# A one-core hybrid attention layer: turning the meta columns behind their step's keys, a mask operand in the first scans, and the last plain gate tiles' weights ahead of the seven-product stage

## The chip, the cores and the metric

The kernel runs on one NeuronCore of a Trainium2 chip. The metric is the device time of one execution in microseconds. The engines that matter are TensorE (PE, and PEld for its weight loads), VectorE (DVE), ScalarE (ACT), GpSimd (POOL) and SyncE (SP), which issues all the DMAs.

## The reference

One decoder layer over 2048 tokens of 1024 features, with 16 learned meta tokens ahead of them. A combined projection gives the queries, keys and values of two attention branches and four sets of gate columns. The first branch is stick-breaking attention with 8 heads: the weight of a key is its sigmoid times the running product of (1 - sigmoid) over all keys between it and the query. The second is sliding-window attention. The branches are gated, projected, merged, and projected out.

```python
xn = rms_norm(h, norm_gain[l])
proj = xn @ w_in[l]
sb_q, sb_k, sb_v, sw_q, sw_k, sw_v, sb_z, sw_z, g_sb, g_sw = jnp.split(proj, offsets, axis=-1)
...
z = jnp.einsum('bqhd,bkhd->bhqk', q[:, q0:end], k[:, :end]) * scale
mask = (s[None, :] < t[:, None]) & valid[None, :end]
log_beta = jax.nn.log_sigmoid(z)
log_1m = jnp.where(mask, log_beta - z, 0.0)
rev = lax.cumsum(log_1m, axis=3, reverse=True)
suffix = jnp.concatenate([rev[..., 1:], jnp.zeros_like(rev[..., :1])], axis=-1)
w = jnp.where(mask, jnp.exp(log_beta + suffix), 0.0)
...
y_sb = (o_sb * jax.nn.silu(sb_z)) @ w_branch_sb[l]
y_sw = (o_sw * jax.nn.silu(sw_z)) @ w_branch_swa[l]
merged = jax.nn.sigmoid(g_sb) * y_sb + jax.nn.sigmoid(g_sw) * y_sw
h = h + merged @ w_out[l]
```

## The kernel before

**Numbers.** Every float32 matrix product is three products of rounded parts: each operand is split into a high part and a low part, and the matmuls are high x high, high x low and low x high. `split` (L105) makes the parts of a weight tile: ScalarE copies the high part (L108) while `hsplit` is set, and VectorE or, while `vsplit` is off, GpSimd subtracts the low part (L111). `evac_split` (L113) does the same with a PSUM bank, ScalarE first (L114), VectorE behind it (L115).

**Order.** The tokens stand in reversed order, so that the running product over the keys is a scan from left to right. They are four groups of 512, worked on in two halves. TensorE's order is the order of the program text. A scheduler orders VectorE, ScalarE, GpSimd and SyncE, except in a few blocks where ScalarE's order is that of the text too; the plain tiles named below are such a block. `weave` mixes two streams on TensorE: projection tiles as the main one, attention steps as the side one.

**Stages of the profiled execution.** To 86 us the start; to 395 us projections and the window attention of the first half; 395 to 640 us the stick-breaking attention of the first half, woven with gate tiles; 640 to 692 us three *plain* gate tiles (`PLAIN`); 692 to 806 us twelve gate tiles (`FAST`) as six pairs by a scheme of seven products; then to 1200 us the window attention and to about 1700 us the stick-breaking attention of the second half, and the final projections.

**A stick step.** `stick` goes through steps of 512 keys by 128 queries (`steps`: head, group, key block n, query tile j). The step s runs `row` for step s, which has two key matmuls (L839) into a bank "z", ScalarE's sigmoid (L843), in the diagonal block (n = 0) a select on GpSimd that sets the masked keys to 1 (L848), and VectorE's scan (L850), the running product. At the last keys of the sequence the 16 meta columns don't fit the bank of 512, so a second pair of matmuls (L841) puts them into the bank "zm", and a second sigmoid (L845) reads that. Five steps (`LT`) later `turn` transposes the rows on TensorE (L861, bank "t", two buffers) and splits them, and `turn_meta` transposes the meta columns of a group's four rows (L872) into the same one bank "zm" and splits that into `wm`. Two steps behind, `values` takes the entries of `av_todo` in order and multiplies by the values (L887, bank "o"); the entry marked `last` ends the sum, which ScalarE and GpSimd read out (L892 to L895). In the step in which a group's last transpose is due, `turn_meta` runs first, then `row`, then `turn`.

**Gate tiles.** A gate tile is 24 matmuls for each group of 512 tokens (`gemm`, L403 to L405) into a bank "g" (two buffers), then ScalarE's sigmoid (L558), for some tiles a product on VectorE (L560), and an output DMA. `lagged` puts the sigmoid of a tile behind the first matmuls of the next.

**Seven products.** `combined` (L925) makes sums of the tokens' parts: its `steps` make t2, t4 (L943 to L952) and t3 (L956), each through `put` (L922 ScalarE, L923 VectorE), a bit of it ahead of each plain tile's group; its `last` puts t1 in place (L963). `pair_weights` (L968) loads and splits the weights of two gate tiles and makes their sums s1 to s4 (L974 to L982). `gate_pairs` (L988) runs, for each pair, seven products of 12 matmuls each (L1000 to L1002) in the order a11·b11, s2·t2, a12·b21, s4·b22, s1·t1, s3·t3, a22·t4, through the banks g, z and t in turn, and adds them up (L1006, the sigmoid is L1009). The weights of the next pair are made at the start of a pair.

Of the kernel before, what the change touches and what calls it, by code (L numbers as in the profile page):

```python
# [7 lines left out]
F32 = mybir.dt.float32  # L8
# [3 lines left out]
ALU = mybir.AluOpType  # L12
# [4 lines left out]
P = 128  # L17
# [5 lines left out]
RW = GT + NM  # L23
NB = SEQ // P
EPS = 1e-6
LT = 5
# [21 lines left out]
def tile_kernel(ctx, tc, x, xt, meta, metat, gain, w_in, w_sb, w_sw, w_out, sinks, fgain,  # L48
# [103 lines left out]
    def drain(*gens):  # L152
        for _ in chain(*gens):
            pass
# [623 lines left out]
    def stick(groups, bp, sums_of={}):  # L778
        kt, vc = {}, {}
        rows_of = {}  # L780
        for g in groups:
# [2 lines left out]
            G.affine_select(out=w, in_=f32(w), pattern=[[-1, 4], [0, P]], compare_op=ALU.is_equal, fill=0.0,  # L784
                            base=-64 - 4 * g, channel_multiplier=1)
        av_todo = []

        def load_kv(h, g):

# [26 lines left out]
        def row(h, g, n, j):  # L816

            if n == j == 0:
                load_kv(h, g)
                state[h, g] = {"q": load_q(h, g), "last": {}}  # L820
                n1 = len(state) - 1
                for g1, ssq in list(sums_of.items())[n1 // 8:n1 // 8 + 1]:
                    i, f = divmod(n1 % 8, 2)
                    t = bp.tile([P, GT], F32, tag="q2", name="xq", bufs=2)
                    DMA(t, x[g1 * GT + i * P:g1 * GT + (i + 1) * P, f * GT:(f + 1) * GT])
                    A.activation(t, t, AF.Square, accum_out=ssq[:, f, i:i + 1])
            st = state[h, g]
            last = st["last"]
            b0 = 4 * (g + n) + j
            nb = min(4, NB - b0)  # L830
            end = b0 + nb == NB
            w = nb * P + (NM if end and nb < 4 else 0)
            k0 = (b0 - 4 * groups[0]) * P
            own = end and nb == 4
            z = ps("z")
            zm = ps("zm") if own else None
            for t, qt in enumerate(st["q"]):
                lq = qt[:, j * P:(j + 1) * P]
                T.matmul(z[:, :w], lhsT=lq, rhs=kt[h][:, k0:k0 + w], start=t == 0, stop=t == 1)  # L839
                if own:  # L840
                    T.matmul(zm[:, :NM], lhsT=lq, rhs=kt[h][:, k0 + w:k0 + w + NM], start=t == 0, stop=t == 1)  # L841
            r = bp.tile([P, RW], F32, tag="row", name="row", bufs=12)
            A.activation(r[:, :w], z[:, :w], AF.Sigmoid, scale=-1.0)  # L843
            if own:
                A.activation(r[:, w:w + NM], zm[:, :NM], AF.Sigmoid, scale=-1.0)  # L845
                w += NM
            if n == 0:
                G.affine_select(out=r[:, :P], in_=r[:, :P], pattern=[[1, P]], compare_op=ALU.is_ge,  # L848
                                fill=1.0, base=-1, channel_multiplier=-1)
            V.tensor_tensor_scan(r[:, :w], r[:, :w], r[:, :w], last[j] if n else 1.0, op0=ALU.mult, op1=ALU.min)  # L850
            last[j] = r[:, w - 1:w]
            rows_of[h, g, n, j] = r

        def turn(h, g, n, i):

            i = 3 - i if n == 0 else i
            nr = i + 1 if n == 0 else 4
            tr = ps("t")
            for j in range(nr):
                k0 = (i - j) % 4 * P  # L860
                T.transpose(tr[:, j * P:(j + 1) * P], rows_of[h, g, n - (j > i), j][:, k0:k0 + P], ident)  # L861
            m = nr * P
            wh = bp.tile([P, GT], F32R, tag="wh", name="wth", bufs=3)
            wl = bp.tile([P, GT], F32R, tag="wl", name="wtl", bufs=3)
            evac_split(wh[:, :m], wl[:, :m], tr[:, :m])
            av_todo.append((h, g, vc[h, g + n][:, i, :], wh[:, :m], wl[:, :m], n == 0 and i == 3, i == (0 if g == 3 else 3) and g + n == 3))

        def turn_meta(h, g):
            p, a = divmod(h, 2)
            tr = ps("zm")  # L870
            for j in range(4):
                T.transpose(tr[:NM, j * P:(j + 1) * P], rows_of[h, g, 3 - g, j][:, GT - P * j:GT - P * j + NM], ident)  # L872
            w = wm[g % 2]
            evac_split(w[0:NM], w[32:32 + NM], tr[:NM])
            av_todo.append((h, g, vm[:, p, a, :], w, None, False, False))

        def values():

            h, g, v, wh, wl, first, last = av_todo.pop(0)
            st = state[h, g]  # L880
            if first:
                st["o"] = ps("o")
            o = st["o"]
            n = wh.shape[1]
            for r in (wh, wl):
                if r is not None:
                    T.matmul(o[:, :n], lhsT=v, rhs=r, start=first and r is wh, stop=last and r is wl)  # L887
            if last:
                p, a = divmod(h, 2)
                t = tmp(rows=64)  # L890
                u = tmp(rows=64)
                A.copy(u, o[0:64])  # L892
                A.copy(t, o[64:128])  # L893
# [5 lines left out]
        n = len(steps)  # L899
        turned = []  # L900
        for s in range(n + LT + 3):
            t = s - LT
            if 0 <= t < n and sum(steps[t][1:3]) == steps[t][3] == 3:
                turn_meta(*steps[t][:2])
                turned.append(s)
                yield 0.43
            if s < n:
                row(*steps[s])
                yield 0.45
            if 0 <= t < n:  # L910
                turn(*steps[t])
                turned.append(s)
                yield 0.43
            while av_todo and turned[0] < s - 1:
                del turned[0]
                yield values()
# [71 lines left out]
    def gate_pairs(ga, gb, pairs, pool, sums_x, between):  # L988
# [7 lines left out]
        def product(a, b):  # L996
            acc = ps("gzt"[next(banks) % 3])
            (wh, wl), (h, l) = a, b
            for k in range(HK):
                T.matmul(acc, lhsT=wh[:, k, :], rhs=h[:, k, :], start=k == 0, stop=False)  # L1000
                T.matmul(acc, lhsT=wh[:, k, :], rhs=l[:, k, :], start=False, stop=False)
                T.matmul(acc, lhsT=wl[:, k, :], rhs=h[:, k, :], start=False, stop=k == HK - 1)  # L1002
            return acc

        def add(t, acc, u):
            V.tensor_tensor(t, acc, u, op=ALU.add)  # L1006
# [2 lines left out]
            A.activation(t, t, AF.Sigmoid)  # L1009
            DMA(dst, t)  # L1010

        nxt = pair_weights(pairs[0][0], pairs[0][2], pool)
        for n, (c, cdst, d, ddst) in enumerate(pairs):
            a11, a12, a22, s1, s2, s3, s4 = nxt
            end = n + 1 == len(pairs)
            if not end:
                nxt = pair_weights(pairs[n + 1][0], pairs[n + 1][2], pool)
            p, u, v, w = (tmp() for _ in range(4))
            A.copy(p, product(a11, b11))
            add(u, product(s2, t2), p)  # L1020
            add(p, product(a12, b21), p)
            gate_out(cdst[ga], p)
            if end:
                between()
            p3 = product(s4, b22)
            p5 = product(s1, t1)
            add(v, p5, u)
            add(v, p3, v)
            gate_out(cdst[gb], v)
            add(u, product(s3, t3), u)  # L1030
            add(w, p5, u)
            gate_out(ddst[gb], w)
            add(u, product(a22, t4), u)
            gate_out(ddst[ga], u)


# [168 lines left out]
    for half, groups in enumerate(halves):  # L1205
# [45 lines left out]
        with tc.tile_pool(name=f"sb{half}", bufs=1, side="left") as bp:  # L1251
# [5 lines left out]
            cost_sb = 8 * sum(4 * (4 - g) for g in groups) * 1.31 + 16 * 0.75  # L1257
            ratio = cost_sb / ((rest - 4) * 10.4)
            weave(tiles_by_tile(gts[4:rest], groups), side, ratio)
            drain(side)  # L1260
            if half == 0:
                t, u = (bp.tile([P, GT], F32, tag="wh", name="sum", bufs=3)[:, :8] for _ in range(2))
# [4 lines left out]
                rs0, rs1 = rs[:, :4], rs[:, 4:]  # L1267
        if half == 0:
            with tc.tile_pool(name="fast", bufs=1, side="left") as bp:
                hsplit[0] = vsplit[0] = True  # L1270
                sums_x = combined(*groups, bp)
                with tc.manual_schedule(engines={mybir.EngineType.Activation}):
                    for mk in gts[rest:-FAST]:
                        w, use, _ = mk()
                        for g in groups:
                            next(sums_x[4], None)
                            drain(lagged(col_tile(w, g, use)))
                    drain(sums_x[4])
                    sums_x[5]()
                places = [(C_GSB + i * P, gs[i]) for i in range(8)] + [(C_GSW + i * P, gw[i]) for i in range(8)]  # L1280
                places = places[-FAST:]
                gate_pairs(*groups, [a + b for a, b in zip(places[::2], places[1::2])], bp, sums_x,
                           lambda: prep(halves[1][0], rs0))
                hsplit[0] = False
        else:
            ringl = rings()
# [65 lines left out]
```

## Time and profile before

| what | value |
| --- | --- |
| median of 3 runs | 2199.65 us (2198.61 to 2199.89) |
| profiled execution | 2202.32 us |
| its span, first to last instruction | 2200.3 us |
| TensorE's mean granted clock in it | 0.994 |
| TensorE busy | 2143.6 us |
| VectorE busy | 1438.8 us |
| ScalarE busy | 1083.8 us |
| GpSimd busy | 340.3 us |

The times of single instructions, waits and stages come from the one profiled execution. A row of the trace's timeline gives the start in microseconds from the start of the span, the duration, engine, line and operation, the tile written and the tiles read, and in brackets the engine's idle time before it with what ended that. A granted clock of 1 is TensorE's full speed.

### The profile page before, as it was taken

The page shows a single profiled execution, that of the slowest core. Times are in us where ns is not written, and L with a number is a line of the kernel's source. Part 1 is how long each engine was busy: PE and PEld are TensorE (multiplying, and loading weights), DVE is VectorE, ACT ScalarE, POOL GpSimd, SP SyncE. Part 2 cuts the span into 40 slices and gives each one's busy share as a digit, 9 for nine tenths or more (in the row PEclk, how much of TensorE's full clock was granted, in tenths as well). Part 3 has the DMA queues.
Part 4 walks back from the last instruction along what each step waited for, and adds up shares of the span by engine and source line. Part 5 has one row for each costly group of instructions (what it writes and reads, how often), then busy time and mean ns, then how long its engine had stood idle before and what let it go on. Part 6 is the DMA issues. An engine that isn't in the chain of part 4 may idle for free.

```text
span 2200.3 us, 30420 instructions
## 1 busy us (share of the span) xinstructions
PE 2143.6 (97%) x10542; PEld 1755.8 (80%) x10542; DVE 1438.8 (65%) x2262; ACT 1083.8 (49%) x2463; POOL 340.3 (15%) x462
## 2 busy tenths in 40 slices
PE   8999999999898999999999999999999999999998
PEld 6788888777676887888887888888888888787886
DVE  7687885567678553677664888887774436454453
ACT  6677774555554333677763555555554312221121
POOL 2233342222210000133220000000000121000000
PEclk9999999999999999999999999999999999999999
DMA  9745546654516665443436333333322985468422
GB/s 333 281 167 192 186 151 214 227 171 153 166 49 232 222 231 193 153 154 135 163 125 192 113 120 120 105 111 115 118 87 91 352 304 182 165 222 286 153 97 86
DMA packets 162617, 380.41 MB, mean 173 GB/s; under 512 B 23168, under 2 KB 24960, under 8 KB 162464
## 3 DMA queue, kind: packets, MB, share of 16 engines
q1 hardware_dynamic: 162464, 378.48, 50.0%
q8 instruction: 83, 1.36, 0.3%
q14 instruction: 70, 0.57, 0.1%
HBM read 237.35 MB, written 140.98 MB: 172 GB/s over the span
## 4 chain that ended last, share of the span: by engine, by line
PE 56%; issue 1%; ACT 1%; DVE 1%; DMA 0%; POOL 0%; SPq 0%; POOLq 0%; ACTq 0%; DVEq 0%
PE ps_g L403 6%; PE ps_g L404 6%; PE ps_g L405 6%; PE ps_o L887 5%; PE ps_z L839 4%; PE ps_t L861 4%; PE ps_g L226 1%; PE ps_g L227 1%; PE ps_z L226 1%; PE ps_z L227 1%; PE ps_z L225 1%; PE ps_g L225 1%; PE ps_o L742 1%; PE ps_z L696 1%; PE ps_t L226 1%
## 5 line engine op out<-in xcount | busy, mean ns | idle before, releaser
L403 PE MATMUL ps_g<-xh,wh 128*128 128x512 f32 x1352 | 556.5, 412 | 17.5 <-ACT wh L108 9.0
L405 PE MATMUL ps_g<-xh,wl 128*128 128x512 f32 x1352 | 533.3, 394 | 0.6 <-DVE wl L111 0.5
L404 PE MATMUL ps_g<-xl,wh 128*128 128x512 f32 x1352 | 532.9, 394 | 0.9 <-DVE xl L379 0.9
L850 DVE TENSOR_TENSOR_SCAN row<-row 128x512 f32<-128x512 f32 (+2 forms) x320 | 370.0, 1159 | 127.1 <-POOL row L848 60.1
L403 PEld LDWEIGHTS ps_g<-xh,wh 128*128 128x128 f32 x1352 | 256.5, 190 | 60.3 <-ACT wh L108 9.8
L405 PEld LDWEIGHTS ps_g<-xh,wl 128*128 128x128 f32 x1352 | 255.2, 189 | 58.8 <-DVE wl L111 1.7
L404 PEld LDWEIGHTS ps_g<-xl,wh 128*128 128x128 f32 x1352 | 256.5, 190 | 42.9 <-DVE xl L379 1.9
L843 ACT ACTIVATE row<-ps_z 128x512 f32<-128x512 f32 (+1 forms) x320 | 171.6, 537 | 193.1 <-PE ps_z L839 151.3
L115 DVE SCALAR_TENSOR_TENSOR wtl<-ps_t,wth 128x512 fp32r<-128x512 f32 (+1 forms) x320 | 188.4, 590 | 28.8 <-ACT wth L114 28.2
L114 ACT ACTIVATE wth<-ps_t 128x512 fp32r<-128x512 f32 (+1 forms) x320 | 170.3, 532 | 63.0 <-PE ps_t L861 62.3
L839 PE MATMUL ps_z<-kt,q 128*128 128x512 f32 (+3 forms) x640 | 188.7, 374 | 0.6 <-ACT row L843 0.6
L861 PE MATMUL ps_t<-ident,row 128*128 128x128 f32 x1088 | 173.5, 274 | 5.4 <-DVE wtl L115 3.1
L861 PEld LDWEIGHTS ps_t<-ident,row 128*128 128x128 f32 x1088 | 135.2, 140 | 42.0 <-DVE wtl L115 6.2
L839 PEld LDWEIGHTS ps_z<-kt,q 128*128 128x128 f32 x640 | 116.8, 189 | 23.3 <-ACT row L843 1.3
L887 PE MATMUL ps_o<-wth,vc 128*128 128x512 f32 (+1 forms) x320 | 130.6, 408 | 1.2 <-ACT tmp L893 0.9
L704 ACT ACTIVATE sc<-sc,nm 128x129 f32<-128x129 f32 x256 | 100.0, 393 | 38.0 <-DVE nm L702 37.4
L887 PE MATMUL ps_o<-wtl,vc 128*128 128x512 f32 (+1 forms) x320 | 117.4, 367 | 0.0
L848 POOL TENSOR_SCALAR_AFFINE_SELECT row<-row 128x128 f32<-128x128 f32 x128 | 44.4, 349 | 411.2 <-ACT row L843 368.3
L111 POOL TENSOR_TENSOR wl<-raw,wh 128x1024 fp32r<-128x1024 f32 (+1 forms) x28 | 60.5, 2160 | 193.2 <-ACT wh L108 176.4
L558 ACT ACTIVATE tmp<-ps_g 128x512 f32<-128x512 f32 x88 | 52.5, 597 | 75.9 <-PE ps_g L405 74.3
L108 ACT CAST wh<-raw 128x1024 fp32r<-128x1024 f32 (+1 forms) x43 | 41.6, 968 | 93.4 <-PE ps_g L226 29.9
L894 POOL TENSOR_TENSOR tmp<-tmp 64x512 f32<-64x512 f32 x32 | 42.8, 1339 | 231.3 <-ACT tmp L893 164.7
(430 smaller groups left out, 3941.6 us busy)
## 6 DMA issues: line engine op xcount, KB each, us to landing
wh<-h_in_w_in SPq DMA_DIRECT2D x66, 512.0 KB, 3.5
wl<-l_in_w_in SPq DMA_DIRECT2D x66, 512.0 KB, 4.7
raw<-in_w_in SPq DMA_DIRECT2D x50, 512.0 KB, 4.9
h_in_w_in<-wh SPq DMA_DIRECT2D x50, 512.0 KB, 2.8
l_in_w_in<-wl SPq DMA_DIRECT2D x50, 512.0 KB, 4.5
q<-qd SPq DMA_DIRECT2D x128, 128.0 KB, 3.1
vc<-vd SPq DMA_DIRECT2D x48, 256.0 KB, 3.6
kd<-tmp SPq DMA_DIRECT2D x32, 256.0 KB, 4.9
```

The source lines that it names most:

```text
L114: A.activation(h, acc, AF.Copy, scale=scale)
L115: V.scalar_tensor_tensor(l, acc, scale, f32(h), op0=ALU.mult, op1=ALU.subtract)
L226: T.matmul(acc, lhsT=wh[:, k, :], rhs=l, start=False, stop=False)
L403: T.matmul(acc, lhsT=wh[:, k, :], rhs=xh[g][:, k, :], start=k == 0, stop=False)
L404: T.matmul(acc, lhsT=wh[:, k, :], rhs=xl[g][:, k, :], start=False, stop=False)
L405: T.matmul(acc, lhsT=wl[:, k, :], rhs=xh[g][:, k, :], start=False, stop=k == KT - 1)
L704: A.activation(sc[:, hh, :], sc[:, hh, :], AF.Exp, bias=nm[:, hh:hh + 1], accum_out=den[:, hh:hh + 1])
L839: T.matmul(z[:, :w], lhsT=lq, rhs=kt[h][:, k0:k0 + w], start=t == 0, stop=t == 1)
L843: A.activation(r[:, :w], z[:, :w], AF.Sigmoid, scale=-1.0)
L850: V.tensor_tensor_scan(r[:, :w], r[:, :w], r[:, :w], last[j] if n else 1.0, op0=ALU.mult, op1=ALU.min)
L861: T.transpose(tr[:, j * P:(j + 1) * P], rows_of[h, g, n - (j > i), j][:, k0:k0 + P], ident)
L887: T.matmul(o[:, :n], lhsT=v, rhs=r, start=first and r is wh, stop=last and r is wl)
```

## The change

The change has four parts.

1. In a stick step, `turn_meta` runs behind `row` and `turn` instead of ahead of them. Its entry in `av_todo` therefore comes after that of `turn`, and it is now the one marked `last`, which ends the sum.
2. In the first half, a tile `mask` of 128 by 528 is made once: ones for the masked keys, which are those of the first 128 columns up to and with the diagonal, and zeros elsewhere. The scan of a diagonal block takes it as its second operand with a maximum, so that masked keys become 1 in the scan itself. GpSimd's select on each of these rows goes away. The second half keeps the select.
3. The weights of the first two plain tiles are loaded and split before the stick steps left over are drained, with ScalarE and VectorE doing the split, and those of the third behind the first tile. The first `pair_weights` call stands behind the third plain tile's first group instead of at the start of `gate_pairs`.
4. In `gate_pairs`, the product a22·t4 is computed ahead of s1·t1, while its sum is still added last.

```diff
+        mask = None
+        if groups[0]:
+            mask = bp.tile([P, RW], F32, name="mask")
+            V.memset(mask[:, P:], 0.0)
+            V.memset(mask[:, :P], 1.0)
+            G.affine_select(out=mask[:, :P], in_=mask[:, :P], pattern=[[-1, P]], compare_op=ALU.is_ge, fill=0.0,
+                            base=0, channel_multiplier=1)
...
-            if n == 0:
+            if n == 0 and mask is None:
                 G.affine_select(out=r[:, :P], in_=r[:, :P], pattern=[[1, P]], compare_op=ALU.is_ge,
                                 fill=1.0, base=-1, channel_multiplier=-1)
-            V.tensor_tensor_scan(r[:, :w], r[:, :w], r[:, :w], last[j] if n else 1.0, op0=ALU.mult, op1=ALU.min)
+            if n == 0 and mask is not None:
+                V.tensor_tensor_scan(r[:, :w], r[:, :w], mask[:, :w], 1.0, op0=ALU.mult, op1=ALU.max)
+            else:
+                V.tensor_tensor_scan(r[:, :w], r[:, :w], r[:, :w], last[j] if n else 1.0, op0=ALU.mult, op1=ALU.min)
...
-            av_todo.append((h, g, vc[h, g + n][:, i, :], wh[:, :m], wl[:, :m], n == 0 and i == 3, i == (0 if g == 3 else 3) and g + n == 3))
+            av_todo.append((h, g, vc[h, g + n][:, i, :], wh[:, :m], wl[:, :m], n == 0 and i == 3, False))
...
-            av_todo.append((h, g, vm[:, p, a, :], w, None, False, False))
+            av_todo.append((h, g, vm[:, p, a, :], w, None, False, True))
...
-                    T.matmul(o[:, :n], lhsT=v, rhs=r, start=first and r is wh, stop=last and r is wl)
+                    T.matmul(o[:, :n], lhsT=v, rhs=r, start=first and r is wh, stop=last)
...
         for s in range(n + LT + 3):
-            t = s - LT
-            if 0 <= t < n and sum(steps[t][1:3]) == steps[t][3] == 3:
-                turn_meta(*steps[t][:2])
-                turned.append(s)
-                yield 0.43
             if s < n:
                 row(*steps[s])
                 yield 0.45
+            t = s - LT
             if 0 <= t < n:
                 turn(*steps[t])
                 turned.append(s)
                 yield 0.43
+                if sum(steps[t][1:3]) == steps[t][3] == 3:
+                    turn_meta(*steps[t][:2])
+                    turned.append(s)
+                    yield 0.43
...
-        nxt = pair_weights(pairs[0][0], pairs[0][2], pool)
         for n, (c, cdst, d, ddst) in enumerate(pairs):
...
             p3 = product(s4, b22)
+            p4 = product(a22, t4)
             p5 = product(s1, t1)
...
-            add(u, product(a22, t4), u)
+            add(u, p4, u)
...
             weave(tiles_by_tile(gts[4:rest], groups), side, ratio)
+            if half == 0:
+                hsplit[0] = vsplit[0] = True
+                plain = [mk() for mk in gts[rest:rest + 2]]
             drain(side)
...
-                hsplit[0] = vsplit[0] = True
                 sums_x = combined(*groups, bp)
                 with tc.manual_schedule(engines={mybir.EngineType.Activation}):
-                    for mk in gts[rest:-FAST]:
-                        w, use, _ = mk()
+                    for n in range(PLAIN):
+                        w, use, _ = plain[n]
                         for g in groups:
-                            next(sums_x[4], None)
+                            if n + 1 < PLAIN:
+                                next(sums_x[4])
                             drain(lagged(col_tile(w, g, use)))
+                            if n + 1 == PLAIN and g == groups[0]:
+                                nxt = pair_weights(pairs[0][0], pairs[0][2], bp)
+                        if n + 2 < PLAIN:
+                            plain.append(gts[rest + n + 2]())
                     drain(sums_x[4])
                     sums_x[5]()
```

More of the change, by code (lines that the diff above doesn't have):

```diff
@@ L986, in pair_weights, with gate_pairs @@
                 s1, s2, s3, s4)
-    def gate_pairs(ga, gb, pairs, pool, sums_x, between):
+    def gate_pairs(ga, gb, pairs, pool, sums_x, nxt, between):
         t1, t2, t3, t4 = sums_x[:4]
```

8 lines of the change are left out of this document (4 added, 4 removed).

## The prediction

> **What bounds the kernel now.** I read the page's busy time first, then a table of stretches, then what TensorE waited for in the stretches where it is not full.
>
> ```profile
> span 2200.3 us, 30420 instructions
> ...
> PE 2143.6 (97%) x10542; PEld 1755.8 (80%) x10542; DVE 1438.8 (65%) x2262; ACT 1083.8 (49%) x2463; POOL 340.3 (15%) x462
> ```
>
> ```profile
> 395.00:640.00 245.00, 224.53 (x1197) 182.62 (x1195) 166.89 (x222) 137.06 (x306) 62.70 (x88) 0.98 0.48 158
> 640.00:692.00 52.00, 42.43 (x180) 33.48 (x180) 40.69 (x64) 21.66 (x33) 2.96 (x3) 0.90 0.35 123
> 692.00:806.00 114.00, 112.52 (x487) 90.69 (x486) 72.78 (x107) 46.33 (x71) 0.00 (x0) 1.00 0.65 232
> 1200.00:1700.00 500.00, 500.00 (x2690) 415.52 (x2689) 389.88 (x464) 274.67 (x533) 38.20 (x76) 1.00 0.34 107
> ```
>
> The second fence is the table of stretches: length, busy time of PE, PEld, DVE, ACT and POOL, granted clock, DMA share, GB/s. TensorE is the bound, 2143.6 of 2200.3 us. Only its holes can be won, 56.7 us, and what it loses at a lowered clock. 20.5 us of hole lie in the first half's stick stretch (395 to 640), 9.6 in the plain tiles (640 to 692), 1.5 in the seven-product stage, none in the second half's stick stretch (1200 to 1700). The change touches just these places. TensorE's waits from 395 to 646 (us in total, times, longest):
>
> ```profile
> PE ps_zm L841 <- DVE wm L115: 14.9, 8, 3.5
> PE ps_t L861 <- DVE wtl L115: 3.1, 5, 0.9
> PE ps_t L861 <- DVE row L850: 0.9, 2, 0.6
> PE ps_o L887 <- ACT tmp L893: 0.9, 1, 0.9
> ```
>
> Once per head the key product of the meta columns (L841) waits for the one bank "zm" until DVE has split the meta weights that were transposed into it just before (L872, L115).
>
> **1. Meta columns behind the keys.** In the first half, one key step of each head needs zm for its own meta keys in the same step in which turn_meta of the group before runs. The two change places: the keys take zm first, and the transposes then wait only for ScalarE's read of it (L845). One collision, and then a key step without one, on PE and on ACT:
>
> ```profile
> 438.61 0.48 PE L839 MATMUL ps_z<-kt,q 128*128 128x512 f32 x1
> 441.16 0.28 PE L841 MATMUL ps_zm<-kt,q 128*128 128x16 f32 x1 [2.07 <-DVE wm L115]
> ```
>
> ```profile
> 419.70 0.39 PE L839 MATMUL ps_z<-kt,q 128*128 128x512 f32 x1
> 419.93 0.17 PE L841 MATMUL ps_zm<-kt,q 128*128 128x16 f32 x1
> ...
> 421.13 0.42 PE L887 MATMUL ps_o<-wth,vc 128*128 128x384 f32 x1
> ```
>
> ```profile
> 421.03 0.18 ACT L845 ACTIVATE row<-ps_zm 128x16 f32<-128x16 f32 x1
> ```
>
> L839 to L841 takes 2.55 us from start to start where 0.23 is usual: 2.32 lost for a listed wait of 2.07, so 0.25 more each. Removed: 14.9 + 8 x 0.25 = 16.9 us. What is late next: in the changed order one gate group (three matmuls) and one transpose always stand between the keys and the meta transposes, as they do before the L887 at 421.13. TensorE would be there at 421.13, and L845 ends at 421.21: 0.1 us, with a restart 0.3, so 8 x 0.3 = 2.4 us remain. Behind the waiting transposes stand value products and the next gate group, for whose results nobody waits at once. Net **14.5 us**. The meta value product (L887 on wm) now closes a group's sum; it has the same two steps' lag as all value products, and of these the list has only the 0.9 us of L893: nothing. In the second half the two fall on different steps and TensorE has no hole: 0, at worst 16 groups at 0.1, 1.6 us.
>
> **2. The clock behind the waits.** Just behind the wait at 441.16:
>
> ```profile
> 442.32 0.63 PE L404 MATMUL ps_g<-xl,wh 128*128 128x512 f32 x1
> ```
>
> It takes 0.63; the key product of the same width at 419.70 took 0.39. The stretches that hold such places:
>
> ```profile
> 440.00:460.00 20.00, 18.59 (x99) 15.62 (x100) 12.54 (x18) 10.31 (x25) 4.93 (x6) 0.91 0.33 113
> 500.00:520.00 20.00, 17.19 (x92) 14.68 (x92) 12.53 (x18) 10.03 (x24) 6.35 (x6) 0.91 0.34 112
> 580.00:600.00 20.00, 15.20 (x75) 11.61 (x75) 14.22 (x20) 10.29 (x23) 4.04 (x7) 0.96 0.53 163
> 600.00:620.00 20.00, 20.00 (x113) 17.16 (x113) 13.46 (x20) 11.21 (x27) 3.54 (x7) 0.95 0.27 93
> ```
>
> Lost: 0.09 x 20 + 0.09 x 20 + (0.04 + 0.05) x 20 = 5.4 us in three places. If the waits cause them, they go. Short waits stay, so I count two of the three: **3.6 us** (0 to 5.4).
>
> [...]
>
> **3. The diagonal mask in the scan.** 64 of the 128 GpSimd selects (L848) go, those of the first half; the mask becomes a second operand of the scan (L850). Added once: two memsets and one select, after the gate product at 372. They hide in DVE's and POOL's idle time between gate tiles:
>
> ```profile
> 378.28 0.69 DVE L560 TENSOR_TENSOR tmp<-ps_g,tmp 128x512 f32<-128x512 f32 x1 [5.47 <-ACT tmp L558]
> 377.83 2.40 POOL L111 TENSOR_TENSOR wl<-raw,wh 128x1024 fp32r<-128x1024 f32 x1 [9.45 <-ACT wh L108]
> ```
>
> Without that cover they would delay a gate tile by about 1 us, once. What the selects cost now (DVE's waits from 395 to 646, and the scans of the whole page):
>
> ```profile
> DVE row L850 <- POOL row L848: 21.8, 31, 3.5
> ```
>
> ```profile
> L850 DVE TENSOR_TENSOR_SCAN row<-row 128x512 f32<-128x512 f32 (+2 forms) x320 | 370.0, 1159 | 127.1 <-POOL row L848 60.1
> ```
>
> DVE gets the 21.8 us back; TensorE sees of it only its own wait on L850 above, **0.9 us**. The scan reads two operands before and after, so I take its 1159 ns unchanged; no row has a mask operand, and the bounds are 0 and a doubling (rival C). Against the gain: with TensorE no longer stopped, DVE must do its 166.89 us in about 225 instead of 245, 74% instead of 68%, and a head's first eight scans are denser than the mean. Some of the old waits return as waits on L115 or L850: beside the 3.1 us that stay I take **-3 us** (0 to -8).
>
> **4. Plain tiles and the first pair.** On PE, ACT and DVE, and one row of the page's DMA part (KB each, us to landing):
>
> ```profile
> 646.96 0.39 PE L403 MATMUL ps_g<-xh,wh 128*128 128x512 f32 x1
> 657.61 0.39 PE L405 MATMUL ps_g<-xh,wl 128*128 128x512 f32 x1
> 665.32 0.80 PE L403 MATMUL ps_g<-xh,wh 128*128 128x512 f32 x1 [7.33 <-ACT wh L108]
> ...
> 711.11 0.39 PE L1000 MATMUL ps_g<-t4h,wh 128*128 128x512 f32 x1
> ...
> 713.91 0.39 PE L1000 MATMUL ps_z<-xh,wh 128*128 128x512 f32 x1
> ```
>
> ```profile
> 658.11 0.62 ACT L922 CAST t4h<-tt 128x512 fp32r<-128x512 f32 x1 [4.88 <-DVE tt L950]
> 658.63 0.59 ACT L558 ACTIVATE tmp<-ps_g 128x512 f32<-128x512 f32 x1
> ```
>
> ```profile
> 664.60 0.69 DVE L956 TENSOR_TENSOR tt<-xl 128x512 f32<-128x512 f32 x1
> 665.30 1.23 DVE L111 TENSOR_TENSOR wl<-raw,wh 128x1024 fp32r<-128x1024 f32 x1
> 666.45 0.68 DVE L923 TENSOR_TENSOR t2l<-tt,t2h 128x512 fp32r<-128x512 f32 x1
> ```
>
> ```profile
> raw<-in_w_in SPq DMA_DIRECT2D x50, 512.0 KB, 4.9
> ```
>
> A plain tile is 48 matmuls, 646.96 to 657.84: 10.9 us. The second tile's split now lies in the stick stretch, so its 7.33 us wait goes; what is late next is the bank. The sigmoid L558 that frees "g" stands on ACT behind t4h, which waits for DVE's L950; it ends at 659.2. Tile two starts at 659.3, 1.4 us late, and tiles two and three run to 681.1; tile three's split is then the one at 665.30, needed at 670.2. On ACT and DVE the moved split (L108, L111) stands ahead of a gate tile's sigmoid and a scan, at most 1.2 us that belong to the range of part 3. On SP the write-backs of that tile move ahead of two output writes, and the next raw load with them; only tmp buffers wait for these: 0, at most 0.5.
>
> A product takes 2.8 us (711.11 to 713.91). Four of the first pair, and then the one pulled ahead (a22 with t4), end at 681.1 + 14.0 = 695.1. The next needs t1, which DVE puts. In the changed order 44 DVE operations stand from L956 at 664.60 to t1's first low part: 5 splits of 1.15 (665.30 to 666.45), and 39 others of 0.6 to 0.73 between the rows above, taken as 0.62: 29.9 us. To this come waits for t4h, for the next pair's raw weights (4.9 us after the first pair's sums let go of them) and for a cast behind the third product, 2.8 together, my estimate. So t1's first part comes from 697.3 to 698.0 and TensorE waits 3 us. 2.6 for the rest of that product and 2.8 for the last put the second pair at 703.5 instead of 713.91: **10.4 us**. At 0.73 an operation it is 6, without any lag of DVE 13.4. Without the pulled-ahead product the wait would be 2.8 longer. Such a wait may lower the clock once: **-1**. After it TensorE is full, so the gain is kept.
>
> **Sum.** 14.5 + 3.6 + 0.9 - 3 + 10.4 - 1 = 25.4 us. The profiled execution took 2202.32 us (its span and 2.0 around it), 2.7 above the median of the runs, 2199.65. So 2202.3 - 25.4 = 2176.9 there, and 2174.3 in the median.
>
> **Rivals.** *A: DVE takes zm's place.* For it: 74% over a whole head leaves little in the dense steps. Against it: no wait on a split is over 0.9 us now, and DVE gets 21.8 us back. Price: 11 us of parts 1 to 3 are not won, gain 14, 2185.5. *B: nothing comes next.* No clock drop, no DVE lag: 14.5 + 5.4 + 0.9 + 13.4 = 34, 2165.5. *C, slower: the scan with a mask operand costs more.* 64 scans at 1159 ns are 74 us. DVE idles 78 us in this stretch; if that can shrink to 25, there is room for 225 - 25 - 167 = 33 us, so from 0.5 us more per scan DVE sets the stretch. Doubled, it lasts 167 + 74 + 25 = 266 instead of 245: 21 lost, 10.4 won, 2210. Against it: the scan already reads two operands. *D: the change does not do what it says*, the collisions stay or turn into equal waits: no change within 0.2%.
>
> **How the numbers follow.** Forecast 0.62 (2168 to 2181), A 0.20, B 0.10, C 0.04, D 0.04. The range reaches from B to just beyond A, 2165.5 to 2186.5; C and D are left out. A measurement of this kernel tells about 0.2% (4.4 us) from no change. Faster is the forecast, A, B and a part of what is between A and D: 0.93; same 0.03, slower 0.04.
>
> **What would show it.** Right: TensorE's waits from 395 to 640 have no meta keys behind wm, only short meta transposes behind ACT; a clock below 1.00 there at most once; the second plain tile waits about 1.4 us for ACT's sigmoid; one wait of 2 to 4 us for t1 before the first pair's sixth product. Wrong: waits on L115 or the scan over 8 us in the stick stretch, a masked scan above 1.7 us, or a second pair that starts as late as before.

## The result, and the profile after

The changed kernel takes 2172.28 us (median of 4 runs, 2169.52 to 2174.90) against 2199.77 us (median of 4), a ratio of 0.9876 with a 95% interval of 0.9859 to 0.9893. It is 27.5 us faster; the forecast was 2174.3 us, 25.4 us faster. Its profiled execution took 2174.90 us, 27.4 less than that of before.

The head of its page, and the table of the same stretches as before (length, busy time of PE, PEld, DVE, ACT and POOL, granted clock, DMA share, GB/s):

```profile
span 2172.9 us, 30212 instructions
...
PE 2135.6 (98%) x10542; PEld 1750.5 (81%) x10542; DVE 1440.5 (66%) x2264; ACT 1083.0 (50%) x2463; POOL 314.9 (14%) x399
```

```profile
395.00:640.00 245.00, 238.41 (x1291) 195.50 (x1290) 189.51 (x254) 148.48 (x323) 40.66 (x27) 1.00 0.51 167
640.00:692.00 52.00, 49.04 (x209) 39.77 (x208) 44.90 (x69) 24.69 (x40) 0.00 (x0) 0.97 0.68 248
692.00:806.00 114.00, 112.60 (x493) 91.36 (x492) 70.09 (x104) 43.36 (x68) 1.54 (x4) 1.00 0.64 225
1200.00:1700.00 500.00, 499.85 (x2660) 415.61 (x2659) 377.04 (x455) 267.95 (x518) 38.06 (x72) 1.00 0.38 121
```

TensorE does the same matmuls in 8.0 us less of busy time (2143.6 before, 2135.6 after), in line with the mean clock of 0.998 instead of 0.994, and its holes shrink from 56.7 to 37.3 us. From 395 to 640 us the hole went from 20.5 to 6.6 us and the clock from 0.98 to 1.00; the changed kernel's row holds 15 us of plain tiles too, so the stages below compare better. TensorE's waits from 395 to 646 us:

```profile
PE ps_t L871 <- DVE wtl L115: 2.3, 3, 1.1
PE ps_o L897 <- ACT tmp L903: 1.8, 6, 0.9
PE ps_g L403 <- ACT tmp L558: 1.5, 1, 1.5
PE ps_t L871 <- DVE row L858: 0.6, 2, 0.3
PE ps_z L846 <- ACT row L850: 0.2, 1, 0.2
```

No wait for the bank "zm" is left: neither the meta keys (now L848, with 14.9 us before, as L841) nor the meta transposes (now L882) are in the list. The lines of the stick steps and the pairs stand 7 to 10 further down in the changed kernel than before. The landmarks of the plain tiles and the first pair on TensorE's timeline:

```profile
399.02 0.39 PE L846 MATMUL ps_z<-kt,q 128*128 128x512 f32 x1
...
624.93 0.39 PE L403 MATMUL ps_g<-xh,wh 128*128 128x512 f32 x1
...
637.48 0.50 PE L403 MATMUL ps_g<-xh,wh 128*128 128x512 f32 x1 [1.51 <-ACT tmp L558]
...
673.24 0.39 PE L1010 MATMUL ps_t<-xh,sh 128*128 128x512 f32 x1
676.59 0.79 PE L1011 MATMUL ps_t<-xl,sh 128*128 128x512 f32 x1 [2.96 <-DVE xl L933]
677.18 0.63 PE L1012 MATMUL ps_t<-xh,sl 128*128 128x512 f32 x1
...
683.45 0.39 PE L1010 MATMUL ps_z<-xh,wh 128*128 128x512 f32 x1
```

The second plain tile waits 1.51 us for the sigmoid that frees its bank, and one wait of 2.96 us for t1 stands in the first pair's sixth product, as the prediction had both. Behind the second wait the matmuls take 0.63 instead of 0.39: the clock is down for about 3.4 us.

From such rows come the lengths of three stages in each profile (us). "Stick" is from the first half's first key product (here 399.02) to the first plain tile (624.93); "first pair" from there to the second pair's first product (683.45); "rest" from the start of the pairs' last matmul to the end of the program's last matmul.

| kernel | stick | first pair | rest |
| --- | --- | --- | --- |
| before | 247.8 | 67.0 | 1381.6 |
| changed | 225.9 | 58.5 | 1384.4 |
| changed, second profile | 224.6 | 57.1 | 1382.7 |

The stick stretch gave 21.9 us, the first pair 8.4 (9.8 in the second profile). A part of the latter is clock: in the kernel before, the plain tiles' wait of 7.33 us was followed by a lowered clock. One row of each profile, before and changed:

```profile
660.00:680.00 20.00, 13.62 (x48) 10.29 (x48) 15.58 (x24) 5.84 (x10) 0.00 (x0) 0.74 0.34 118
```

```profile
660.00:680.00 20.00, 17.04 (x67) 13.43 (x67) 18.36 (x28) 9.87 (x16) 0.00 (x0) 0.91 0.79 287
```

Lost are 0.26 x 20 = 5.2 us before and 0.09 x 20 = 1.8 after, so 3.4 of the 8.4 us are clock; in the changed kernel's second profile, with 1.00 in this row, it is 5.2 of the 9.8.

At the first key product of the second half, the changed kernel is 30.3 us ahead (1183.21 and 1152.88). It loses 0.5 in the second half's stick stretch and 2.2 in the last 450 us. The 0.5 goes with the first part of the change: from its first to its last key product that stretch takes 493.6 us in the three kernels with the meta transposes ahead of the keys, and 494.1 to 494.3 in the nine profiles with them behind. The 2.2 is spread: the code there is the same, and the twelve profiles of this case lie between 448.9 and 451.5 us, the changed kernel's first at the top.

### The profile page after: what moved, and what is told of

Same layout as the page of the kernel before. It is cut to its first block, busy times and chain, and to the rows that moved or that the text cites. A ratio compares the mean times of both kernels' runs of the same rounds, so it can differ in the third digit from the quotient of the medians.

```text
span 2172.9 us, 30212 instructions
## 1 busy us (share of the span) xinstructions
PE 2135.6 (98%) x10542; PEld 1750.5 (81%) x10542; DVE 1440.5 (66%) x2264; ACT 1083.0 (50%) x2463; POOL 314.9 (14%) x399
## 4 chain that ended last, share of the span: by engine, by line
PE 81%; DVE 6%; ACT 5%; DMA 4%; issue 3%; POOL 1%; SPq 0%; DVEq 0%; ACTq 0%; POOLq 0%
PE ps_g L403 11%; PE ps_g L404 11%; PE ps_g L405 11%; PE ps_o L897 6%; PE ps_z L846 6%; PE ps_t L871 5%; PE ps_o L742 2%; PE ps_z L696 2%; PE ps_g L227 1%; PE ps_g L226 1%; PE ps_g L225 1%; PE ps_z L227 1%; PE ps_z L225 1%; PE ps_z L226 1%; PE ps_t L227 1%
## 5 line engine op out<-in xcount | busy, mean ns | idle before, releaser
L860 DVE TENSOR_TENSOR_SCAN row<-row 128x512 f32<-128x512 f32 (+4 forms) x256 | 303.2, 1186 | 93.9 <-ACT row L850 48.7
L115 DVE SCALAR_TENSOR_TENSOR wtl<-ps_t,wth 128x512 fp32r<-128x512 f32 (+1 forms) x320 | 188.0, 588 | 21.9 <-ACT wth L114 21.7
L858 DVE TENSOR_TENSOR_SCAN row<-row,mask 128x512 f32<-128x512 f32 (+2 forms) x64 | 73.2, 1149 | 22.7 <-ACT row L850 18.7
```

The costliest lines, as they stand in the source:

```text
L115: V.scalar_tensor_tensor(l, acc, scale, f32(h), op0=ALU.mult, op1=ALU.subtract)
L858: V.tensor_tensor_scan(r[:, :w], r[:, :w], mask[:, :w], 1.0, op0=ALU.mult, op1=ALU.max)
```

## Experiments

All edits are to the changed kernel unless the text says otherwise. Each ratio is to the kernel before, run beside it on the same chip. The changed kernel's own two ratios are 0.9876 and, in the second set, 0.9866.

**The meta columns' transposes back ahead of the keys**, with the flags of their entries as before.

```diff
+            t = s - LT
+            if 0 <= t < n and sum(steps[t][1:3]) == steps[t][3] == 3:
+                turn_meta(*steps[t][:2])
...
             if s < n:
                 row(*steps[s])
...
-                if sum(steps[t][1:3]) == steps[t][3] == 3:
-                    turn_meta(*steps[t][:2])
```

> The changed kernel with the meta columns' transposes ahead of their step's keys again, all else as changed. Theory (the one bank zm, and the clock that falls behind the waits): eight waits of the meta key product on the weights' split come back, 14.9 us by the list of before, 2 of restart and up to 5.4 of lowered clock, so 17 to 22 us more than the changed kernel, 2190 to 2195; the granted clock of the stretch falls below 1.00 in two or three places. Rival (the mask and the split's relief of VectorE brought a part of it, since the split that the key product waits for is VectorE's): the waits come back at half, 8 to 11 us more, 2180 to 2184.

Measured: 2188.02 us, ratio 0.9942 (0.9927 to 0.9957), 14 to 17 us more than the changed kernel. TensorE's waits from 395 to 720 us:

```profile
PE ps_zm L848 <- DVE wm L115: 13.7, 8, 3.2
PE ps_t L1011 <- DVE xl L933: 2.9, 1, 2.9
PE ps_t L871 <- DVE wtl L115: 2.4, 6, 0.7
```

The eight waits are back at nearly their old size, which rules out the rival. The stick stretch is 244.2 us, 18 to 20 longer, as the theory has it: 13.7 of wait, 2 of restart, and 3.4 of clock, which fell in two places of this stretch (0.97 and 0.95 in neighbouring stretches of 20 us, 0.91 in a third). The total is 2 us below the theory's range. The missing part is not in the stretch: the second half's stick stretch is 0.5 shorter with the old order, the first pair takes 56.8 us without a fall of the clock, and the rest takes 1382.4 us, which lies within the spread of the profiles.

**The selects back in place of the mask.**

```diff
-        if groups[0]:
+        if False:
             mask = bp.tile([P, RW], F32, name="mask")
```

> The changed kernel with GpSimd's select on each diagonal row of the first half instead of the mask operand. Theory (TensorE saw only 0.9 us of the selects): 1 to 3 us more than the changed kernel, 2173 to 2176, with VectorE's wait on the select back at about 20 us and TensorE's waits on the scan and on the transposed weights' split at 4 to 6 us instead of 2.9. Rival (with the collisions gone VectorE sets the stretch, so the 20 us it waits count): 8 us or more, above 2180, and the waits on the split above 10 us.

Measured: 2171.73 us, ratio 0.9863 (0.9848 to 0.9878): no difference from the changed kernel. VectorE's longest waits from 395 to 640 us, and two of TensorE's from 395 to 720:

```profile
DVE row L860 <- POOL row L855: 24.9, 26, 3.0
```

```profile
PE ps_t L871 <- DVE wtl L115: 2.2, 4, 0.9
...
PE ps_t L871 <- DVE row L860: 0.9, 2, 0.6
```

VectorE waits 24.9 us for the selects and TensorE 0.9 us for the scans, 0.3 more than with the mask. TensorE's waits on the scan and the split are 3.1 us together, below the 4 to 6 of the theory, and the time is below its range too. The stick stretch is 226.3 us against 225.9 and 224.6. The mask is worth 0.4 to 1.6 us in the stretch, and nothing that the time shows.

**The plain tiles' and the first pair's weights made where they were before.**

```diff
-            if half == 0:
-                hsplit[0] = vsplit[0] = True
-                plain = [mk() for mk in gts[rest:rest + 2]]
             drain(side)
...
+                hsplit[0] = vsplit[0] = True
                 sums_x = combined(*groups, bp)
...
-                        w, use, _ = plain[n]
+                        w, use, _ = gts[rest + n]()
...
-                            if n + 1 == PLAIN and g == groups[0]:
-                                nxt = pair_weights(pairs[0][0], pairs[0][2], bp)
...
+                nxt = pair_weights(pairs[0][0], pairs[0][2], bp)
                 gate_pairs(*groups, pairs, bp, sums_x, nxt, lambda: prep(halves[1][0], rs0))
```

> The changed kernel with the plain tiles' weights and the first pair's weights made where they were before; the product of a22 with t4 stays ahead. Theory: the second plain tile waits about 7 us for its weights' split again, the third about 1.7, and the second pair starts about 8.4 us later, 2179 to 2183. Rival (in the changed order VectorE's work for t1 sets the start of the second pair anyway, so that making the weights ahead only moves the wait): 3 us or less, with the wait for t1 gone to zero.

Measured: 2178.01 us, ratio 0.9894 (0.9877 to 0.9911). TensorE's waits from 620 us to 700:

```profile
PE ps_g L403 <- ACT wh L108: 9.2, 2, 7.5
PE ps_z L1012 <- DVE sl L992: 0.9, 1, 0.9
PE ps_z L1010 <- ACT sh L991: 0.6, 1, 0.6
```

The first pair's stage is 67.7 us, 9 to 10.5 longer, and the wait for t1 is gone. So the weights ahead of time did not only move the wait. About 5 us of the stage are clock again, which is at 0.91 and 0.83 from 620 to 660 us. A price of the weights ahead of time is not shown: with the splits back, the stick stretch is 224.2 us, but other kernels with the splits in it have 224.3 to 225.9. The total is 4 to 6 us above the changed kernel, 1 us below the theory's range, with intervals of 4 us on each side; the stage shows more than the time, because the rest is 2.2 to 4 us shorter in this profile, which is spread.

**The product of a22 with t4 last again.**

```diff
-            p4 = product(a22, t4)
             p5 = product(s1, t1)
...
-            add(u, p4, u)
+            add(u, product(a22, t4), u)
```

> The changed kernel with the product of a22 with t4 last again. Theory: t1 comes no earlier, and the product that needs it stands one product of 2.8 us earlier, so the wait for t1 in the first pair grows from 3.0 to about 5.8 us and the time by 2.8, 2174 to 2177. Rival (t1 is held up by TensorE's own order or by the bank, so the wait stays at 3 us): no difference.

Measured: 2173.31 us, ratio 0.9874 (0.9859 to 0.9889). The time shows no difference; the interval would also allow 3 us. The trace does show one:

```profile
PE ps_z L1011 <- DVE xl L933: 3.1, 1, 3.1
PE ps_z L1010 <- ACT xh L932: 2.1, 1, 2.1
```

The waits for t1 add up to 5.2 us instead of 3.0, and the first pair's stage is 62.4 us, 4 to 5 longer: 2.2 of that is wait, and most of the remainder clock, which is at 0.88 and 0.95 from 660 to 700 us (3.4 us lost, against 1.8 and none). The wait grows by less than the 2.8 expected. The theory holds in its stage; in the total it is not shown.

**The changed kernel again.**

> The changed kernel once more, as the ground for the other runs of this set. By its own first runs 0.9876 of the kernel before, about 2173; the stick-breaking stretch of the first half 226 us from its first key product to the first plain tile's. A second profile also shows whether the lowered clock behind the wait for t1 comes each time (theory: no, two kernels with the same wait kept the full clock; rival: yes, 1.4 to 1.7 us each time).

Measured: 2169.51 us, ratio 0.9866 (0.9852 to 0.9881), and 224.6 us for the stretch. The wait for t1 is 3.0 us again, but this time the clock stays at 1.00 in every stretch from 400 to 720 us. The two kernels above with waits of 2.9 and 3.0 us at the same place also kept it there.

**The second pair's weights behind t1.**

```diff
                     sums_x[5]()
+                    second = pair_weights(pairs[1][0], pairs[1][2], bp)
...
-            if not end:
+            if n == 0:
+                nxt = second
+            elif not end:
                 nxt = pair_weights(pairs[n + 1][0], pairs[n + 1][2], pool)
```

> The changed kernel with the second pair's weights made behind t1 on ScalarE (in the same hand order), so that on VectorE two of their splits of 1.2 us, two sums of 0.6, one addition of 0.6 and an idle time of 1.6 no longer stand ahead of t1. Theory (VectorE's queue alone holds t1 up): t1 comes 5.7 us earlier, the wait of 3.0 and the lowered clock behind it vanish, the second pair starts 3 to 4.7 us earlier, 2168 to 2170. Rival (the work put off is as urgent): the second pair's first product waits for its own weights' split instead, and the time stays within 1 us of the changed kernel.

Measured: 2165.12 us, ratio 0.9847 (0.9832 to 0.9862), 4.4 us less than the changed kernel beside it. VectorE's timeline at t1's low parts, first in the changed kernel, then here, where they stand ahead of the second pair's splits, and TensorE at the sixth product:

```profile
675.85 2.49 DVE L933 TENSOR_TENSOR xl<-xs,xh 128x512 fp32r<-128x512 f32 x4
```

```profile
668.52 2.49 DVE L933 TENSOR_TENSOR xl<-xs,xh 128x512 fp32r<-128x512 f32 x4
670.93 2.35 DVE L111 TENSOR_TENSOR wl<-raw,wh 128x1024 fp32r<-128x1024 f32 x2
```

```profile
670.41 0.39 PE L1010 MATMUL ps_t<-xh,sh 128*128 128x512 f32 x1
670.65 0.39 PE L1011 MATMUL ps_t<-xl,sh 128*128 128x512 f32 x1
```

Counted from the first plain tile, t1's low parts begin at 46.4 us instead of 50.9: 4.5 earlier, where 5.7 were expected. There is no wait at t1, and TensorE's list of waits from 655 to 800 us is empty. The first pair's stage is 53.8 us, 3.3 shorter, as expected, and the second pair does not wait for its weights, which rules out the rival; the time is 3 us below the theory's range, which was counted from 2173 us too. The second pair's work that stood ahead of t1 had held it up. This version beats both kernels.

**Only the transposes moved, on the kernel before.** The edit is the first part of the change with its three flags.

> The kernel before with nothing changed but the place of the meta columns' transposes. Theory (the parts of the stick-breaking stretch overlap little, the collisions carry 14.9 of wait, 2 of restart and up to 5.4 of clock): the stretch goes from 247.8 to 225 or 226 us, the plain tiles and the first pair keep their 67 us, 2177 to 2180. Rival (the mask is needed to let VectorE keep up): the stretch stays above 230, with waits on the split above 8 us, 2183 or more.

Measured: 2181.41 us, ratio 0.9919 (0.9902 to 0.9937). The waits from 395 to 646 us:

```profile
PE ps_g L403 <- ACT wh L108: 7.6, 1, 7.6
PE ps_t L861 <- DVE wtl L115: 2.5, 2, 1.5
PE ps_o L887 <- ACT tmp L893: 1.2, 3, 0.9
PE ps_t L861 <- DVE row L850: 0.9, 2, 0.6
```

The stick stretch is 226.3 us, 21.5 shorter by this one edit, and VectorE keeps up without the mask. In time it is worth 16.5 us, 1.4 less than the theory's range allows. A part of the difference is in the first pair's stage, which takes 69.4 instead of 67.0 us, with the clock at 0.98, 0.77 and 0.92 from 620 to 680 where the kernel before has 1.00, 1.00 and 0.74: 6.6 us lost instead of 5.2. The remainder lies within the spread of the runs.

**More VectorE work in the stick stretch.**

```diff
+            again = bp.tile([P, RW], F32, name="again")
...
                 V.tensor_tensor_scan(r[:, :w], r[:, :w], mask[:, :w], 1.0, op0=ALU.mult, op1=ALU.max)
+                V.tensor_tensor(again[:, :w], r[:, :w], mask[:, :w], op=ALU.max)
```

> The changed kernel with one more VectorE operation of about 0.62 us, whose result nobody reads, behind each of the 64 scans with a mask: 40 us more of VectorE work where the stretch of 226 us has 51 us of VectorE idle. The prediction's rival C set 0.5 us per scan as the point from which VectorE decides, on the estimate that its idle time can't fall below 25 us. By that estimate: 175 + 40 + 25 = 240, 14 us more, 2186 to 2188. Rival (the idle time can be filled): 0 to 4 us more, 2173 to 2177. A third outcome, VectorE's dense steps don't share their load with the others: more than 20 us.

Measured: 2180.83 us, ratio 0.9919 (0.9904 to 0.9934), 11.3 us more than the changed kernel beside it. The stick stretch as one row of the table, first of the changed kernel's second profile, then of this one:

```profile
397.90:622.50 224.60, 220.64 (x1214) 181.40 (x1213) 175.63 (x230) 142.38 (x315) 38.70 (x25) 1.00 0.54 174
```

```profile
397.70:635.30 237.60, 223.28 (x1214) 182.96 (x1213) 211.83 (x294) 144.02 (x315) 41.16 (x25) 0.99 0.52 164
```

```profile
PE ps_t L873 <- DVE wtl L115: 11.2, 11, 2.7
```

VectorE's busy time in the stretch grew by 36.2 us. The stretch is 13.0 us longer where 14 were expected, and the total 11.3; the time is 5 us below the range expected, which was counted from 2173 us and not from the 2169.5 of the changed kernel beside it. VectorE's idle time in the stretch fell from 49.0 to 25.8 us, and the prediction had set 25 as the least; that it can't fall further with more work is not shown by this one amount. TensorE's new waits are those on the split of the transposed weights. So in the changed kernel VectorE could take up about half of its idle time, and the remainder of the added work made the stretch longer.

**The tokens' sums behind their plain tile's group**, in the version with the second pair's weights behind t1.

```diff
-                            if n + 1 < PLAIN:
-                                next(sums_x[4])
                             drain(lagged(col_tile(w, g, use)))
+                            if n + 1 < PLAIN:
+                                next(sums_x[4])
```

> The version with the second pair's weights behind t1, and besides it each step of the tokens' sums put behind its plain tile's group instead of ahead of it, so that on ScalarE the sigmoid which frees the bank of the second plain tile stands ahead of the cast of t4. Theory: the wait of 1.5 us for that sigmoid goes, t1 has 1.5 us of slack in that version and still comes in time, so 1.5 us less than 0.9847 of the kernel before: 0.984. Rival (the sums come later now, and with them t1): the 1.5 us come back as a wait for t1 or t2, 0.985 or more.

Measured: 2168.44 us, ratio 0.9852 (0.9836 to 0.9869): no better than without it. The wait for the sigmoid is gone, but these have come:

```profile
PE ps_t L1010 <- ACT xh L932: 1.0, 1, 1.0
PE ps_t L1011 <- DVE xl L933: 1.0, 2, 0.7
```

The rival was right: the sums came later, and t1 with them. Counted from the first plain tile, VectorE begins t1's low parts at 48.4 us instead of 46.4.

**Only the mask, on the kernel before.** The edit is the second part of the change.

> The kernel before with nothing changed but the mask operand in the first half's first scans. Theory (TensorE saw only 0.9 us of the selects; the eight collisions end with VectorE's split, which may come a little earlier): the stretch from the first key product to the first plain tile 244 to 247 instead of 247.8 us, the eight waits for the bank at 13.5 to 14.9 us, 2196 to 2200, 0.9985 or so. Rival (the 21.8 us that VectorE waited for the selects count while the collisions are there): 5 us or more, the waits for the bank below 12 us.

Measured: 2198.30 us, ratio 0.9987 (0.9977 to 0.9997). The waits for the bank from 395 to 642 us:

```profile
PE ps_zm L848 <- DVE wm L115: 13.5, 8, 3.2
```

The waits go from 14.9 to 13.5, as expected and against the rival, which had them below 12. The stretch is 242.0 us, 5.8 shorter, and 2 us below the range expected. Of the 5.8 us, 3.6 are clock: in this profile it fell in one place of the stretch (0.91 over 20 us, 1.8 us) and in that of before in three (5.4 us). A wait of 2.9 to 3.0 us at one place was followed by a fall in two profiles and by none in three (last section), so it may be luck, and no run settles it; the time says 3 us with an interval from 0.7 to 5.

## Why the prediction was right, step by step

- **Part 1, the collisions (14.5).** Right in mechanism, too small in size. The 14.9 us of wait went, and of the 2.4 us that were to remain at the meta transposes nothing did: L882 is in no list of waits. Moved alone, the transposes shorten the stretch by 21.5 us. The 14.9, the clock's 5.4 and 0.3 less of other waits make 20.6, which leaves about 1 us for the restarts, half of the 2.0 counted. The 0.5 us that the second half lost lies within the 0 to 1.6 that were set for it.
- **Part 2, the clock (3.6).** All 5.4 went. Both profiles of the changed kernel show 1.00 from 400 to 640 us. One place of three had been kept for the short waits that stay; they cost no clock.
- **Part 3, the mask and VectorE's pace (0.9 - 3).** This is the term that failed. The -3 was for waits on VectorE that would return once TensorE was no longer stopped. They fell instead, from 4.0 us on L115 and the scan to 2.9 and, in the second profile, 1.8. VectorE's 78% of the new stretch, with 49 us idle, was not dense enough to stop TensorE; only the added work, which left 25.8 us idle, brought such waits. The 0.9 lies within the 0.4 to 1.6 that the mask gives.
- **Part 4, plain tiles and first pair (10.4 - 1).** 8.4 in one profile, 9.8 in the other. The bank's wait was 1.51 (1.4 was worked out), the wait for t1 2.96 (3). The count behind it held as well: in the changed kernel's timeline 44 VectorE operations, five of them splits, stand from L966 at 642.80 to t1's low parts at 675.85, 33.05 us where 29.9 and 2.8 were set. Putting the second pair's weights behind t1 removed the wait. The lowered clock came in one profile of two and then cost 1.8 us, not 1. What the prediction does not name is that 3.4 to 5.2 us of this gain are the clock that the kernel before lost behind its wait of 7.33 us; the working counts all later matmuls at full speed, and so has them in its 10.4.
- **Sum.** Parts 1 to 3 made 16.0 us and were 21.9; part 4 made 9.4 and was 8.4; 2.7 were lost behind it, in stages to which I gave 0, mostly spread. 25.4 against 27.4 in the profiled executions. The mechanism of each part but the -3 is what the runs show; that the sum is right to 2 us is partly luck, because the under-estimate of the stretch and the loss at the end partly cancel.
- **Rivals.** A (VectorE takes the bank's place) needs waits on L115 that are not there; it begins with the added work, which brought 11.2 us of them. B (nothing comes next) describes the stick stretch, where its terms add up to 20.8 us, but not the first pair, where t1 was waited for. C did not come: a masked scan that runs alone takes 1.22 us, like the others. One sign of being wrong did appear, a masked scan above 1.7 us: eight of the 64 took 1.79 to 2.42 us. Each began inside a GpSimd operation (see below), and the mask was not their cause. D did not come: the eight waits are gone.

## What to carry to other kernels

When two uses of a single bank meet in one step, look at which of them has its result waited for soonest: here a change of order brought 21.5 us of stretch for 14.9 us of listed wait, because restarts (about 1 us) and the lowered clock behind three of the waits (5.4 us) went with it. An engine's waits are worth what the bounding engine waits for them: 24.9 us of VectorE's waiting for selects showed on TensorE as 0.9 us of waiting for scans, of which 0.6 stay without the selects. Ahead of a hand-over, count the instructions in the producer's queue and put those for later products behind it; here the work for the next pair, which the scheduler had put ahead, was what the consumer waited for.

## What the runs showed of the hardware

**The same wait does not always cost clock.** Waits for t1 of 2.9 to 3.0 us at the same place were followed by a lowered clock in one profile of the changed kernel and in the kernel with more VectorE work, and by 1.00 in the changed kernel's second profile and in two variants. In the kernel before, three of eight collisions were followed by a lowered clock.

In the kernel before, the lowered stretches begin at 441.5, 502.9, 598.5 and 660.0 us and last 3.4 us, the last one 10.2; the distances between them are 18, 28 and 18 times 3.41 us. Taking that as a grid, here are two of its stretches in the changed kernel, and two in its second profile, where the grid is counted back from the lowered clock behind the last matmul:

```profile
673.00:676.40 3.40, 0.63 (x3) 0.19 (x1) 3.40 (x6) 1.52 (x3) 0.00 (x0) 1.00 0.76 249
676.40:679.80 3.40, 3.21 (x8) 2.54 (x9) 3.40 (x6) 1.68 (x2) 0.00 (x0) 0.50 0.98 374
```

```profile
669.00:672.40 3.40, 2.26 (x10) 1.50 (x8) 3.40 (x6) 3.02 (x6) 0.00 (x0) 1.00 0.48 186
672.40:675.80 3.40, 1.59 (x7) 1.31 (x8) 3.40 (x6) 0.42 (x1) 0.00 (x0) 1.00 0.96 323
```

The wait that fell into one stretch left TensorE idle for 81% of it, and the next stretch is at half clock. The wait of the same length that lay across two left it idle for 34 and 53%, and cost nothing. From 90 to 2140 us of the twelve profiles the clock falls from full to half 15 times. In 14 of them TensorE had been idle for 56% or more of the grid stretch just before; of all the stretches that were not followed by a fall, the idlest had 56% too. One fall, at 676.7 us in the kernel with only the transposes moved, follows a stretch with 48%. In the kernel before, the four falls follow stretches with 56, 57, 61 and 79%, and the idlest of its other stretches at full clock had 48%; in the changed kernel's first profile these are 81 and 44%. So in these profiles the falls stand, but for one, behind stretches in which TensorE was idle for more than half, and the two waits above left their stretches idle for different shares because they began at different places in the grid. Why the clock falls there is not shown.

Over the runs the falls show in the means: granted clock 0.993 to 0.997 before, 0.998 to 0.999 after.

**A scan beside a GpSimd operation ends late.** The 128x512 scans with the mask averaged longer than those of the same shape without it (the first row is the changed kernel, the second the one with the selects back):

```profile
L858 DVE TENSOR_TENSOR_SCAN row<-row,mask 128x512 f32<-128x512 f32 x32 | 42.7, 1337 | 15.2 <-ACT row L850 15.0
```

```profile
L860 DVE TENSOR_TENSOR_SCAN row<-row 128x512 f32<-128x512 f32 x32 | 39.8, 1247 | 17.0 <-POOL row L855 16.8
```

The mask is not the reason. Three rows of the changed kernel's timeline, two of VectorE and one of GpSimd:

```profile
428.97 1.22 DVE L858 TENSOR_TENSOR_SCAN row<-row,mask 128x512 f32<-128x512 f32 x1 [0.54 <-ACT row L850]
...
436.24 1.81 DVE L858 TENSOR_TENSOR_SCAN row<-row,mask 128x512 f32<-128x512 f32 x1 [1.26 <-ACT row L850]
```

```profile
435.66 1.30 POOL L904 TENSOR_TENSOR tmp<-tmp 64x512 f32<-64x512 f32 x1 [8.13 <-ACT tmp L903]
```

The scan that began inside the GpSimd operation (435.66 to 436.96) took 0.59 us longer than the one that ran alone. Of the 32 masked scans of this shape, the 25 that began outside GpSimd's operations took 1.19 to 1.23 us, and the seven that began inside one took 1.53 to 1.85. All seven ended 1.08 to 1.09 us behind the end of the GpSimd operation, the one above at 438.05, though they had begun 0.53 to 0.84 us after its start. What held them up is not shown. With the selects gone, other scans fall beside these operations than before. In TensorE's waits these longer scans do not show: those on the scans are 0.6 us.
